# The second product of a streaming layer: x rounded ahead of the weights, block products in another order, the shared sum and the layer norm sums spread over more steps

## The chip, the cores and the metric

One core of one Trainium2 chip runs the kernel in one launch. The metric is the device time of that launch in microseconds, the median over runs of the same program.

## What is computed

One encoder layer over 1056 rows (1024 of a prompt, 32 of a running stream). The change concerns its last part, the second product of the MLP and the layer norm behind it. The reference, cut to that:

```python
x = _layernorm(ALPHA * x + mix, ln1_g, ln1_b)
hid = jax.nn.relu(x @ w_ff1)                    # (1056, 1024) @ (1024, 4096)
ff = (hid * hid) @ w_ff2                        # (1056, 4096) @ (4096, 1024)
x = _layernorm(ALPHA * x + ff, ln2_g, ln2_b)
```

Everything is float32. A float32 operand goes through TensorE as a rounded part and a remainder, and a product of two operands as three matmuls (`three`): rounded by rounded, rounded by remainder, remainder by rounded.

## The kernel before

**Block products.** The 4096 hidden features are 32 tiles of 128. Tiles 14, 15, 30 and 31 (`CLASSIC`) go through plain products. The other 28 make 14 pairs, and each pair's product with the weights is done as seven block products in place of eight (Winograd's form of Strassen's scheme). The weights of a pair are four blocks of 128 x 512, `A["11"]`, `A["12"]`, `A["21"]`, `A["22"]`; the columns are two halves of 528 (`H`), each two quarters of 264 (`Q`). The sums of hidden blocks that the seven products need were written to DRAM (`hd`) by the first product.

**Groups and steps.** `ff2_chunk` makes the steps of one group of pairs (groups of 5, 5 and 4). A product is one step for each pair: 4 tiles of outputs (d) by 2 quarters by 3 matmuls, 24 matmuls. The products stand in the order P1, P2, P6, P7, P4, P5, P3. P1 and P2 add into the same four accumulators (`acc`, two PSUM banks each; four of them are all that there are), P7 and P4 into the same four, P5 and P3 into the same four; P6 has four alone. P6 takes weights n2 = A21 + A22 - A11 (two additions, L1033 and L1034, which leave n1 and n2 behind), P7 takes A11 - A21, P3 takes A12 - n2 (one addition each, `add_w`, L853); P1, P2, P4 and P5 take blocks that are there.

**What a step has.** `load` (DMAs, all issued on SP's queue), `prep`, `mm` and `post`. `prep` of a product forms the weights on DVE, rounds them on ACT (L108) and takes the remainder on POOL (L111), then rounds the hidden block x on ACT and takes its remainder on DVE (L111). `post` of a product's last step takes the four accumulators out: `keep` adds them to the shared sum u (on DVE L1002; in the first group, for P1, a copy on ACT, L1000), `add_z` adds them to the output tiles `zz` (L1009, L1011). P1 and P6 go to u.

**The order of the work.** `run` writes the program out: at step i the loads of step i + 6, the preps up to step i + 3, then the matmuls and the post of step i. Each engine and SP's queue work through their own rows in exactly that order (`manual_schedule`). The rounded x lies in a ring of four slots, so the prep of step i + 3 waits for the matmuls of step i - 1; the rounded weights have six.

**The last group.** After P4 of the last group the program turns to quarters of columns: `qs[q]` are eight plain steps for quarter q (12 matmuls each), M5 is P5 in four steps (one for each d, 24 matmuls), M3 is P3 in two times four steps (12 matmuls each). They stand in the order qs[0], qs[1], M5, M3[0], qs[2], M3[1], qs[3]. `fold` adds u to three of the four quadrants of the output: quadrant (m, half) with m the half of the features. It stands in the posts of P7, one of the three additions on DVE and two on POOL. u's four parts lie in `w_b` and `w_c`; these tiles are used again afterwards for plain weights (`ew`) and for P3's.

**The second layer norm.** Quarters 0 to 2 use `ln2_parts`, whose pieces hang in the posts of later steps: `total` (three additions on POOL, L1225), `centre` (a small sum on TensorE, L1208, four subtractions on DVE, L1232, four squares on ACT and three additions on POOL, L1238), `root` (a small sum, L1208, then L1243 and L1244), and twice `scaled_out` (four of L1214 on DVE, four of L1215 on ACT, the output DMAs). Quarter 3 is `last_quarter`.

**Other lines that are spoken of:** `load_z` (L988) brings the tiles `zz` (1056 KB each) into buffers that `ff1_steps` used; L939 and L941 write the last sums of a pair of the first product to `hd`. L1126 and L1131 add the accumulators of M5 and M3, L1258 those of the plain steps.

Of the kernel before, what the change touches and what calls it, by code (L numbers as in the profile page):

```python
# [69 lines left out]
def hybrid_layer(ctx, tc, xT, win, wkw, wo, w1, w2, ckT, cv, ckiT, scT, cw, lnp, rb, cst, oh,  # L70
# [940 lines left out]
                    V.tensor_tensor(zs, accs[d], zs, op=OP.add)  # L1011
        return f

    def fold(d):

        def f():
            for i, (m, half) in enumerate(((1, 0), (1, 1), (0, 1))):
                zs = z_half(4 * m + d, half)
                (V if i == 0 else G).tensor_tensor(zs, zs, rings2["u"].parts[d], op=OP.add)
        return f  # L1020

    def ff2_chunk(ci, pairs):
# [14 lines left out]
        def product(loads, form, to, xn, post):  # L1037
            first = to.islower()
            to = to.lower()
            out = []  # L1040
            for i, p in enumerate(pairs):
                got = {}

                def load_x(p=p, got=got):
                    got["x"] = hidden_raw()
                    nc.sync.dma_start(got["x"], hd[p, FORM[xn]])

                def prep(p=p, got=got):
                    got["w"] = split_w(form(p))
                    hl = xhl.next().rearrange("p (a b) -> p a b", a=2)  # L1050
                    split(got["x"], hl[:, 0], hl[:, 1], lo_eng=V)
                    got["x"] = hl

                def mm(i=i, got=got):
                    if first and i == 0:
                        accs[to] = [new_acc() for _ in range(4)]
                    hl, x = got["w"], got["x"]
                    for d in range(4):
                        wh, wl = (hl[:, a, d * 128:d * 128 + 128] for a in range(2))
                        for c in range(2):  # L1060
                            cols = slice(c * Q, c * Q + Q)
                            three(accs[to][d][:, c], wh, wl, x[:, 0, cols], x[:, 1, cols],
                                  first and i == 0, i == len(pairs) - 1, not first)

                out.append(Step([load_a(n, p) for n in loads] + [load_x], [prep], [mm]))
            out[-1].post.append(lambda: post(accs[to]))
            return out

        def by_features(form, xn, place, post, groups):
# [9 lines left out]
            def prep(*ps):  # L1079
                def f():  # L1080
                    raw = [form(p) for p in ps]
                    for p, r in zip(ps, raw):
                        w, x = place(pairs.index(p))
                        split(r, *w)
                        split(got[p]["raw"], *x, lo_eng=V)
                        got[p]["w"], got[p]["x"] = w, x
                return f

# [39 lines left out]
        def post3(d, acc, cs):  # L1128
            for c in cs:
                zs = z_half(d, 1)[:, c * Q:c * Q + Q]  # L1130
                V.tensor_tensor(zs, acc[:, c], zs, op=OP.add)  # L1131

        P1 = product(["11"], lambda p: A["11", p], "a", "11", lambda a: keep(a, ci, True))
        P2 = product(["12"], lambda p: A["12", p], "A", "21", add_z(0, 0, ci == 0))
        P6 = product(["21", "22"], form_s2, "b", "t2", lambda a: keep(a, ci, False))
        P7 = product([], lambda p: add_w(A["11", p], A["21", p], OP.subtract), "c", "t3", add_z(1, 1, ci == 0))
        P4 = product([], lambda p: A["22", p], "C", "t4", add_z(1, 0, ci == 0))
        if ci == len(PAIRS) - 1:
            P5 = by_features(lambda p: n1[p], "t1", place5, post5, [(p,) for p in pairs])
            P3 = by_features(lambda p: add_w(A["12", p], n2[p], OP.subtract), "22", place3, post3, [pairs[:1], pairs[1:2], pairs[2:]])  # L1140
            return P1, P2, P6, P7, P4, P5, P3
# [76 lines left out]
    def ln2_parts(c0, n):  # L1218
        cols = slice(c0, c0 + n)
        got = {}  # L1220

        def total():
            got["s1"] = unit("s1")
            for i in range(1, 4):
                G.tensor_tensor(got["s1"], z[0][:, :, cols] if i == 1 else got["s1"], z[i][:, :, cols], op=OP.add)  # L1225

        def centre():
            mean = small_sum([(ones, got["s1"][:, a]) for a in range(2)])
# [11 lines left out]
        def root():  # L1240
# [2 lines left out]
            S.activation(got["rstd"], var, AF.Sqrt, bias=eps)  # L1243
            V.reciprocal(got["rstd"], got["rstd"])  # L1244

        return (total, centre, root, lambda: scaled_out(c0, n, got["rstd"], range(4)),
                lambda: scaled_out(c0, n, got["rstd"], range(4, 8)))

    def plain_step(q, d):
# [11 lines left out]
    def plain(q):  # L1261
        return [plain_step(q, d) for d in range(8)]
# [64 lines left out]
    n = len(steps)  # L1327
    for ci, pairs in enumerate(PAIRS):
        P1, P2, P6, P7, P4, P5, P3 = ff2_chunk(ci, pairs)
        steps += P1 + P2 + P6 + P7 + P4  # L1330
        if ci < len(PAIRS) - 1:
            steps += P5 + P3
    for i in range(4):
        steps[n + (2, 3, 8, 9)[i]].load.append(load_z(i))
    for j in range(8):
        load, prep = classic_x(j % 4, j // 4)
        steps[n + 36 + 4 * j].load.append(load)
        steps[n + 36 + 4 * j].prep.append(prep)
    for j in range(4):
        P7[j].post.insert(0, fold(j))  # L1340
    qs = [plain(0), plain(1), plain(2), last_quarter()]
    (load5, prep5, step5), (load3, prep3, step3) = P5, P3
    M5 = [step5(d, (0, 1)) for d in range(4)]
    M3 = [[step3(d, (c,)) for d in range(4)] for c in range(2)]
    steps += qs[0] + qs[1] + M5 + M3[0] + qs[2] + M3[1] + qs[3]
    for j in range(4):
# [4 lines left out]
        qs[0][5 + j // 2].load.append(load5[j])  # L1351
        qs[1][3 + j].prep.append(prep5[j])
        M5[1 + j // 2].load.append(load3[j])
    M5[3].prep += prep3
    for q, when in ((0, (qs[1][0], qs[1][3], qs[1][6], M5[0], M5[1])),
                  (1, (M5[0], M5[2], M3[0][1], qs[2][0], qs[2][2])),
                  (2, (M3[1][0], M3[1][3], qs[3][2], qs[3][4], qs[3][5]))):
        for f, st in zip(ln2_parts(q * Q, Q), when):
            st.post.append(f)
    with tc.manual_schedule(engines=ORDERED):  # L1360
# [84 lines left out]
```

## Time and profile before

| | |
|---|---|
| median of 3 runs | 1383.65 us (1382.64 to 1383.94) |
| the profiled execution: its own time, its span | 1387.17 us, 1385.4 us |
| PE busy | 1256.0 us, 91% of the span |
| DVE busy | 996.7 us, 72% |
| ACT busy | 691.6 us, 50% |
| POOL busy | 565.8 us, 41% |

The profile is of one execution. Times in it count from the start of its span, in microseconds. PE, DVE, ACT, POOL and SP are TensorE, VectorE, ScalarE, GpSimd and SyncE; L1002 is line 1002 of the kernel before. A wait is named by the instruction that waited and the one that released it. The granted clock of TensorE is given as a share of full speed (1.00 is 2.4 GHz, 0.50 is 1.2 GHz).

### The profile page before, as it was taken

The page shows a single profiled execution, that of the slowest core. Times are in us where ns is not written, and L with a number is a line of the kernel's source. Part 1 is how long each engine was busy: PE and PEld are TensorE (multiplying, and loading weights), DVE is VectorE, ACT ScalarE, POOL GpSimd, SP SyncE. Part 2 cuts the span into 40 slices and gives each one's busy share as a digit, 9 for nine tenths or more (in the row PEclk, how much of TensorE's full clock was granted, in tenths as well). Part 3 has the DMA queues.
Part 4 walks back from the last instruction along what each step waited for, and adds up shares of the span by engine and source line. Part 5 has one row for each costly group of instructions (what it writes and reads, how often), then busy time and mean ns, then how long its engine had stood idle before and what let it go on. Part 6 is the DMA issues. An engine that isn't in the chain of part 4 may idle for free. (4 is left out here: it accounts for less than half of the span.)

```text
span 1385.4 us, 24095 instructions
## 1 busy us (share of the span) xinstructions
PE 1256.0 (91%) x8822; PEld 1213.8 (88%) x8822; DVE 996.7 (72%) x2039; ACT 691.6 (50%) x1378; POOL 565.8 (41%) x456
## 2 busy tenths in 40 slices
PE   7999999898899979777999999999889989988794
PEld 6999999897788969666999999999889979978784
DVE  5675899999588898789276667667565665675666
ACT  5676989544688788755222221223333434333224
POOL 2412344432511333455344454554343434438522
PEclk9999999999999999997999999999999989999997
DMA  6320111135521212242143443447734724622111
GB/s 199 97 68 30 46 47 40 49 113 173 148 55 24 69 39 47 80 137 96 60 163 122 151 155 137 143 156 249 272 82 123 239 79 117 210 75 81 36 60 63
DMA packets 97223, 149.99 MB, mean 108 GB/s; under 512 B 12456, under 2 KB 41808, under 8 KB 97104
## 3 DMA queue, kind: packets, MB, share of 16 engines
q1 hardware_dynamic: 81664, 139.55, 31.2%
q0 software_dynamic: 9504, 4.33, 1.8%
q10 hardware_dynamic: 5936, 4.58, 1.2%
q8 instruction: 69, 1.13, 0.4%
q14 instruction: 50, 0.41, 0.1%
HBM read 105.41 MB, written 43.00 MB: 107 GB/s over the span
## 5 line engine op out<-in xcount | busy, mean ns | idle before, releaser
L111 POOL TENSOR_TENSOR whl<-wraw,whl 128x512 fp32r<-128x512 f32 (+1 forms) x184 | 247.7, 1351 | 459.8 <-ACT whl L108 434.5
L858 PE MATMUL acc<-b,whl 128*128 128x264 f32 x1088 | 317.2, 292 | 30.9 <-DVE w_b L1002 11.9
L859 PE MATMUL acc<-b,whl 128*128 128x264 f32 x1088 | 315.8, 290 | 0.0
L860 PE MATMUL acc<-b,whl 128*128 128x264 f32 x1088 | 314.0, 289 | 0.0
L858 PEld LDWEIGHTS acc<-b,whl 128*128 128x128 f32 x1088 | 211.1, 194 | 33.3 <-issue 30.2
L108 ACT ACTIVATE whl<-wraw 128x512 fp32r<-128x512 f32 (+1 forms) x184 | 113.3, 624 | 230.8 <-DVE wraw L853 200.0
L860 PEld LDWEIGHTS acc<-b,whl 128*128 128x128 f32 x1088 | 211.4, 194 | 0.0
L859 PEld LDWEIGHTS acc<-b,whl 128*128 128x128 f32 x1088 | 210.7, 194 | 0.1
L131 PE MATMUL mm<-xh,whl 128*128 128x384 f32 (+4 forms) x520 | 172.5, 332 | 15.5 <-ACT whl L108 5.6
L132 PE MATMUL mm<-area,whl 128*128 128x384 f32 (+4 forms) x552 | 182.4, 331 | 0.4 <-DVE area L111 0.4
L111 DVE TENSOR_TENSOR b<-xraw,b 128x528 fp32r<-128x528 f32 x94 | 104.7, 1117 | 103.3 <-ACT b L108 99.8
L133 PE MATMUL mm<-xh,whl 128*128 128x384 f32 (+4 forms) x520 | 170.0, 332 | 0.0
L441 ACT ACTIVATE junka<-s,cand 128x1024 bf16<-128x1024 f32 (+1 forms) x93 | 96.5, 1037 | 41.8 <-DVE cand L454 34.0
L131 PEld LDWEIGHTS mm<-xh,whl 128*128 128x128 f32 (+1 forms) x520 | 98.2, 189 | 19.3 <-issue 8.1
L132 PEld LDWEIGHTS mm<-area,whl 128*128 128x128 f32 (+1 forms) x552 | 104.3, 189 | 3.0 <-DVE area L111 0.8
L111 POOL TENSOR_TENSOR whl<-at,whl 128x512 fp32r<-128x512 f32 x56 | 79.0, 1420 | 53.9 <-ACT whl L108 53.9
L133 PEld LDWEIGHTS mm<-xh,whl 128*128 128x128 f32 (+1 forms) x520 | 97.6, 188 | 3.2 <-POOL whl L111 1.2
L108 ACT ACTIVATE b<-xraw 128x528 fp32r<-128x528 f32 x94 | 59.9, 638 | 65.9 <-PE acc L860 47.6
L443 DVE TENSOR_SCALAR_CACHE_REDUCE junk<-s,cand 128x384 bf16<-128x384 f32 (+1 forms) x124 | 80.3, 648 | 1.3
L858 PE MATMUL acc<-area,whl 128*128 128x264 f32 x240 | 68.4, 285 | 0.0
L859 PE MATMUL acc<-area,whl 128*128 128x264 f32 x240 | 68.1, 284 | 0.0
L860 PE MATMUL acc<-area,whl 128*128 128x264 f32 x240 | 68.0, 283 | 0.0
(310 smaller groups left out, 3317.9 us busy)
## 6 DMA issues: line engine op xcount, KB each, us to landing
hd<-ring SPq DMA_DIRECT2D x98, 264.0 KB, 2.1
xraw<-hd SPq DMA_DIRECT2D x98, 264.0 KB, 2.7
at<-in_w_dram SPq DMA_DIRECT2D x58, 256.0 KB, 3.7
wraw<-in_win_dram SPq DMA_DIRECT2D x52, 256.0 KB, 2.6
wraw<-in_wo_dram SPq DMA_DIRECT2D x40, 256.0 KB, 2.7
w_a<-in_w_dram SPq DMA_DIRECT2D x23, 256.0 KB, 3.5
w_c<-in_w_dram SPq DMA_DIRECT2D x19, 256.0 KB, 4.6
zz<-zd SPq DMA_DIRECT2D x4, 1056.0 KB, 9.1
```

Source lines behind the costliest of these rows:

```text
L108: S.activation(hi, raw, AF.Copy)
L111: (lo_eng or G).tensor_tensor(lo, raw, f32(hi), op=OP.subtract)
L131: PE.matmul(ps, wh[k], a, start=(k == 0), stop=False)
L132: PE.matmul(ps, wh[k], b, start=False, stop=False)
L133: PE.matmul(ps, wl[k], a, start=False, stop=(k == K - 1))
L441: S.activation(junk(R, N), s, AF.Sign, bias=c, scale=-1.0, accum_out=cnt[:R, i:i + 1])
L443: V.tensor_scalar(junk(R, N), s, c, -float(k), op0=OP.is_ge, op1=OP.add, accum_out=cnt[:R, i:i + 1])
L858: PE.matmul(ps, wh, xhi, start=start, stop=False, skip_group_check=more)
L859: PE.matmul(ps, wh, xlo, start=False, stop=False, skip_group_check=more)
L860: PE.matmul(ps, wl, xhi, start=False, stop=stop, skip_group_check=more)
```

## The change

In the preps x is rounded ahead of the weights. In the first two groups P6 moves behind P7 and P4, and the loads of A21 and A22 move from P6 to P7 and P4; the last group keeps its order. The first two output tiles are loaded three steps earlier. The additions of u to the output move from the posts of P7 to those of P4, and eight of the twelve are on DVE now (before four). `total` is cut into three pieces that hang in the quarter's own steps, the other layer norm pieces move by some steps, and the preps of P3 in the last group hang in three steps in place of one.

```diff
--- before.py
+++ after.py
@@ -1011,12 +1011,11 @@
                     V.tensor_tensor(zs, accs[d], zs, op=OP.add)
         return f
 
-    def fold(d):
+    def fold(d, m, half, eng):
 
         def f():
-            for i, (m, half) in enumerate(((1, 0), (1, 1), (0, 1))):
-                zs = z_half(4 * m + d, half)
-                (V if i == 0 else G).tensor_tensor(zs, zs, rings2["u"].parts[d], op=OP.add)
+            zs = z_half(4 * m + d, half)
+            eng.tensor_tensor(zs, zs, rings2["u"].parts[d], op=OP.add)
         return f
 
     def ff2_chunk(ci, pairs):
@@ -1046,10 +1045,10 @@
                     nc.sync.dma_start(got["x"], hd[p, FORM[xn]])
 
                 def prep(p=p, got=got):
-                    got["w"] = split_w(form(p))
+                    raw = form(p)
                     hl = xhl.next().rearrange("p (a b) -> p a b", a=2)
                     split(got["x"], hl[:, 0], hl[:, 1], lo_eng=V)
-                    got["x"] = hl
+                    got["x"], got["w"] = hl, split_w(raw)
 
                 def mm(i=i, got=got):
                     if first and i == 0:
@@ -1081,8 +1080,8 @@
                     raw = [form(p) for p in ps]
                     for p, r in zip(ps, raw):
                         w, x = place(pairs.index(p))
+                        split(got[p]["raw"], *x, lo_eng=V)
                         split(r, *w)
-                        split(got[p]["raw"], *x, lo_eng=V)
                         got[p]["w"], got[p]["x"] = w, x
                 return f
 
@@ -1130,12 +1129,13 @@
                 zs = z_half(d, 1)[:, c * Q:c * Q + Q]
                 V.tensor_tensor(zs, acc[:, c], zs, op=OP.add)
 
+        ends = ci == len(PAIRS) - 1
         P1 = product(["11"], lambda p: A["11", p], "a", "11", lambda a: keep(a, ci, True))
         P2 = product(["12"], lambda p: A["12", p], "A", "21", add_z(0, 0, ci == 0))
-        P6 = product(["21", "22"], form_s2, "b", "t2", lambda a: keep(a, ci, False))
-        P7 = product([], lambda p: add_w(A["11", p], A["21", p], OP.subtract), "c", "t3", add_z(1, 1, ci == 0))
-        P4 = product([], lambda p: A["22", p], "C", "t4", add_z(1, 0, ci == 0))
-        if ci == len(PAIRS) - 1:
+        P6 = product(["21", "22"] if ends else [], form_s2, "b", "t2", lambda a: keep(a, ci, False))
+        P7 = product([] if ends else ["21"], lambda p: add_w(A["11", p], A["21", p], OP.subtract), "c", "t3", add_z(1, 1, ci == 0))
+        P4 = product([] if ends else ["22"], lambda p: A["22", p], "C", "t4", add_z(1, 0, ci == 0))
+        if ends:
             P5 = by_features(lambda p: n1[p], "t1", place5, post5, [(p,) for p in pairs])
             P3 = by_features(lambda p: add_w(A["12", p], n2[p], OP.subtract), "22", place3, post3, [pairs[:1], pairs[1:2], pairs[2:]])
             return P1, P2, P6, P7, P4, P5, P3
@@ -1219,10 +1219,11 @@
         cols = slice(c0, c0 + n)
         got = {}
 
-        def total():
-            got["s1"] = unit("s1")
-            for i in range(1, 4):
+        def total(i):
+            def f():
+                got["s1"] = unit("s1")
                 G.tensor_tensor(got["s1"], z[0][:, :, cols] if i == 1 else got["s1"], z[i][:, :, cols], op=OP.add)
+            return f
 
         def centre():
             mean = small_sum([(ones, got["s1"][:, a]) for a in range(2)])
@@ -1243,7 +1244,7 @@
             S.activation(got["rstd"], var, AF.Sqrt, bias=eps)
             V.reciprocal(got["rstd"], got["rstd"])
 
-        return (total, centre, root, lambda: scaled_out(c0, n, got["rstd"], range(4)),
+        return (total(1), total(2), total(3), centre, root, lambda: scaled_out(c0, n, got["rstd"], range(4)),
                 lambda: scaled_out(c0, n, got["rstd"], range(4, 8)))
 
     def plain_step(q, d):
@@ -1327,18 +1328,23 @@
     n = len(steps)
     for ci, pairs in enumerate(PAIRS):
         P1, P2, P6, P7, P4, P5, P3 = ff2_chunk(ci, pairs)
-        steps += P1 + P2 + P6 + P7 + P4
         if ci < len(PAIRS) - 1:
-            steps += P5 + P3
+            steps += P1 + P2 + P7 + P4 + P6 + P5 + P3
+        else:
+            steps += P1 + P2 + P6 + P7 + P4
     for i in range(4):
-        steps[n + (2, 3, 8, 9)[i]].load.append(load_z(i))
+        steps[n + (-1, 0, 8, 9)[i]].load.append(load_z(i))
     for j in range(8):
         load, prep = classic_x(j % 4, j // 4)
         steps[n + 36 + 4 * j].load.append(load)
         steps[n + 36 + 4 * j].prep.append(prep)
     for j in range(4):
-        P7[j].post.insert(0, fold(j))
+        d = (j + 3) % 4
+        P4[j].post[:0] = [fold(d, 1, 0, V), fold(d, 1, 1, G)]
     qs = [plain(0), plain(1), plain(2), last_quarter()]
+    P4[0].post.append(fold(3, 0, 1, V))
+    for d in range(3):
+        P4[1 + d].post.insert(0, fold(d, 0, 1, V))
     (load5, prep5, step5), (load3, prep3, step3) = P5, P3
     M5 = [step5(d, (0, 1)) for d in range(4)]
     M3 = [[step3(d, (c,)) for d in range(4)] for c in range(2)]
@@ -1351,10 +1357,12 @@
         qs[0][5 + j // 2].load.append(load5[j])
         qs[1][3 + j].prep.append(prep5[j])
         M5[1 + j // 2].load.append(load3[j])
-    M5[3].prep += prep3
-    for q, when in ((0, (qs[1][0], qs[1][3], qs[1][6], M5[0], M5[1])),
-                  (1, (M5[0], M5[2], M3[0][1], qs[2][0], qs[2][2])),
-                  (2, (M3[1][0], M3[1][3], qs[3][2], qs[3][4], qs[3][5]))):
+    for f, st in zip(prep3, (M5[3], M3[0][0], M3[0][1])):
+        st.prep.append(f)
+    for q, when in ((0, (qs[1][2], qs[1][7], M5[0], M5[1])),
+                    (1, (M5[1], M3[0][3], qs[2][2], qs[2][5])),
+                    (2, (M3[1][1], qs[3][1], qs[3][2], qs[3][3]))):
+        when = (qs[q][3], qs[q][5], qs[q][7]) + when
         for f, st in zip(ln2_parts(q * Q, Q), when):
             st.post.append(f)
     with tc.manual_schedule(engines=ORDERED):
```

The ACT row, at the fourth and fifth step of the first group's P2 (b_6874 is the ring of rounded x, whl_6870 that of rounded weights, xraw_6872 the loaded x, w_b the loaded A12). Before:

```order
L108 ACTIVATE whl_6870<-w_b 128x512
L108 ACTIVATE b_6874<-xraw_6872 128x528
L1000 ACTIVATE w_b<-acc 128x528 x3
L1000 ACTIVATE w_c<-acc 128x528
L108 ACTIVATE whl_6870<-w_b 128x512
L108 ACTIVATE b_6874<-xraw_6872 128x528
```

Now:

```order
L108 ACTIVATE b_6874<-xraw_6872 128x528
L108 ACTIVATE whl_6870<-w_b 128x512
L1000 ACTIVATE w_b<-acc 128x528 x3
L1000 ACTIVATE w_c<-acc 128x528
L108 ACTIVATE b_6874<-xraw_6872 128x528
L108 ACTIVATE whl_6870<-w_b 128x512
```

In each prep the rounding of x has moved ahead of the rounding of the weights.

DVE's row in the last group, from P7's last steps to P4's (zz are output tiles, two features tiles each; L1019 and L1018 are the additions of u, L1011 the adding of accumulators, L111 the remainder of x). Before:

```order
L1019 TENSOR_TENSOR zz_10814<-zz_10814,w_b 128x528
L111 TENSOR_TENSOR b_6874<-xraw_6872,b_6874 128x528
L1019 TENSOR_TENSOR zz_10814<-zz_10814,w_b 128x528
L111 TENSOR_TENSOR b_6874<-xraw_6872,b_6874 128x528
L1019 TENSOR_TENSOR zz_10846<-zz_10846,w_b 128x528
L111 TENSOR_TENSOR b_6874<-xraw_6872,b_6874 128x528
L1019 TENSOR_TENSOR zz_10846<-zz_10846,w_c 128x528
L1011 TENSOR_TENSOR zz_10814<-acc,zz_10814 128x528 x2
L1011 TENSOR_TENSOR zz_10846<-acc,zz_10846 128x528 x2
L111 TENSOR_TENSOR b_6874<-xraw_6872,b_6874 128x528
```

Now:

```order
L111 TENSOR_TENSOR b_6874<-xraw_6872,b_6874 128x528
L1018 TENSOR_TENSOR zz_10846<-zz_10846,w_c 128x528
L1018 TENSOR_TENSOR zz_10547<-zz_10547,w_c 128x528
L1018 TENSOR_TENSOR zz_10514<-zz_10514,w_b 128x528
L1018 TENSOR_TENSOR zz_10814<-zz_10814,w_b 128x528
L1018 TENSOR_TENSOR zz_10514<-zz_10514,w_b 128x528
L1018 TENSOR_TENSOR zz_10814<-zz_10814,w_b 128x528
L1018 TENSOR_TENSOR zz_10547<-zz_10547,w_b 128x528
L1018 TENSOR_TENSOR zz_10846<-zz_10846,w_b 128x528
L1011 TENSOR_TENSOR zz_10814<-acc,zz_10814 128x528 x2
L1011 TENSOR_TENSOR zz_10846<-acc,zz_10846 128x528 x2
```

Four additions that stood between preps ahead of P7's post are eight now, in one piece, ahead of P4's post. POOL has four of the twelve now.

DVE's row at M5 (L1244 and L1245 are the reciprocals of a layer norm's root, at and w_b hold weights, area gets P3's rounded x). Before, from the reciprocal of quarter 0 on:

```order
L1244 RECIPROCAL at<-at 128x264
L1258 TENSOR_TENSOR zz_10846<-acc,zz_10846 128x264
L853 TENSOR_TENSOR wraw_6871<-w_b,at 128x512
L111 TENSOR_TENSOR area<-xraw_6872,area 128x528
L853 TENSOR_TENSOR wraw_6871<-w_b,at 128x512
L111 TENSOR_TENSOR area<-xraw_6872,area 128x528
L853 TENSOR_TENSOR wraw_6871<-w_b,at 128x512 x2
L111 TENSOR_TENSOR area<-xraw_6872,area 128x528 x2
L1126 TENSOR_TENSOR zz_10814<-acc,zz_10814 128x528
L1126 TENSOR_TENSOR zz_10608<-acc,zz_10608 128x528
L1214 SCALAR_TENSOR_TENSOR zz_10608<-zz_10608,lnw,at 128x264 x2
L1214 SCALAR_TENSOR_TENSOR zz_10640<-zz_10640,lnw,at 128x264 x2
```

Now, from the prep of P3's second pair on (L1125 is the line that was L1126, L1233 the one that was L1232):

```order
L853 TENSOR_TENSOR wraw_6871<-w_b,at 128x512
L111 TENSOR_TENSOR area<-xraw_6872,area 128x528
L1125 TENSOR_TENSOR zz_10814<-acc,zz_10814 128x528
L1125 TENSOR_TENSOR zz_10514<-acc,zz_10514 128x528
L1214 SCALAR_TENSOR_TENSOR zz_10814<-zz_10814,lnw,at 128x264 x2
L1214 SCALAR_TENSOR_TENSOR zz_10846<-zz_10846,lnw,at 128x264 x2
L1233 TENSOR_TENSOR zz_10514<-zz_10514,acc 128x2x264
L1233 TENSOR_TENSOR zz_10547<-zz_10547,acc 128x2x264
L1233 TENSOR_TENSOR zz_10814<-zz_10814,acc 128x2x264
L1233 TENSOR_TENSOR zz_10846<-zz_10846,acc 128x2x264
L853 TENSOR_TENSOR wraw_6871<-w_b,at 128x512 x2
L111 TENSOR_TENSOR area<-xraw_6872,area 128x528 x2
```

Before, all four preps of P3 (L853 and L111) stood ahead of M5's first post; now two pairs stand behind two posts, eight of L1214 and the centring of quarter 1.

## Rows read from the trace of the kernel before

**Rows 1.** Waits of PE, 990 to the end: total, times, longest, us

```profile
PE acc L858 <- DVE w_b L1002: 11.9, 3, 4.3
PE acc L858 <- DVE zz L1011: 11.2, 5, 4.4
PE acc L1208 <- POOL w_d L1225: 7.8, 1, 7.8
PE acc L1208 <- DVE w_d L1282: 6.4, 1, 6.4
PE acc L858 <- DVE zz L1009: 5.4, 1, 5.4
PE acc L1208 <- POOL w_d L1238: 5.2, 3, 2.2
```

**Rows 2.** Windows: length, busy PE, PEld, DVE, ACT, POOL, granted clock, DMA share, GB/s

```profile
1065.62:1109.76 44.14, 44.13 (x360) 43.93 (x360) 29.99 (x36) 18.08 (x32) 20.10 (x14) 1.00 0.70 222
...
1256.40:1262.25 5.85, 5.85 (x26) 5.85 (x27) 2.89 (x4) 0.00 (x0) 5.85 (x6) 0.50 0.00 0
sum 26.99, PE 26.98 PEld 26.99 DVE 19.03 ACT 5.08 POOL 9.12; mean PE 4.50 PEld 4.50 DVE 3.17 ACT 0.85 POOL 1.52
```

**Rows 3.** Timeline of the last group's P6 and P7 preps: start, duration, instruction

```profile
1214.33 0.69 DVE L1034 TENSOR_TENSOR at<-w_d,w_a 128x512 f32<-128x512 f32 x1
1216.32 1.37 DVE L111 TENSOR_TENSOR b<-xraw,b 128x528 fp32r<-128x528 f32 x1 [1.29 <-ACT b L108]
1218.32 0.69 DVE L1034 TENSOR_TENSOR at<-w_d,w_a 128x512 f32<-128x512 f32 x1
1231.28 0.68 DVE L853 TENSOR_TENSOR wraw<-w_a 128x512 f32<-128x512 f32 x1
1234.53 0.68 DVE L853 TENSOR_TENSOR wraw<-w_a 128x512 f32<-128x512 f32 x1
...
1215.12 0.63 ACT L108 ACTIVATE whl<-at 128x512 fp32r<-128x512 f32 x1 [2.82 <-DVE at L1034]
1215.66 0.63 ACT L108 ACTIVATE b<-xraw 128x528 fp32r<-128x528 f32 x1
```

**Rows 4.** Groups by line, 900 to the end: count, busy us, mean ns, idle before

```profile
L1034 DVE TENSOR_TENSOR at<-w_d,w_a 128x512 f32<-128x512 f32 x14 | 9.7, 692 | 0.5
L1011 DVE TENSOR_TENSOR zz<-acc,zz 128x528 f32<-128x528 f32 x36 | 23.3, 698 | 9.6 <-PE acc L860 7.7 <-POOL zz L1019 1.9
L1019 POOL TENSOR_TENSOR zz<-zz,w_c 128x528 f32<-128x528 f32 x2 | 2.6, 1308 | 0.0
L1244 DVE RECIPROCAL at<-at 128x264 f32<-128x264 f32 x3 | 5.4, 1803 | 10.3 <-ACT at L1243 10.3
L1214 DVE SCALAR_TENSOR_TENSOR zz<-zz,lnw,at 128x264 f32<-128x264 f32 x32 | 15.6, 552 | 0.0
```

**Rows 5.** Timeline of POOL and DVE at P7 of the last group

```profile
1242.88 3.55 POOL L1019 TENSOR_TENSOR zz<-zz,w_b 128x528 f32<-128x528 f32 x2
...
1243.42 1.83 DVE L1019 TENSOR_TENSOR zz<-zz,w_b 128x528 f32<-128x528 f32 x1
1245.17 1.82 DVE L111 TENSOR_TENSOR b<-xraw,b 128x528 fp32r<-128x528 f32 x1
```

**Rows 6.** Timeline of PE: the first matmul of the last group's P4

```profile
1256.40 0.56 PE L858 MATMUL acc<-b,whl 128*128 128x264 f32 x1 [4.43 <-DVE zz L1011]
```

**Rows 7.** Windows: the end of qs[1], and M5 to the first step of M3

```profile
1297.33:1299.79 2.46, 2.46 (x13) 2.46 (x12) 1.70 (x1) 0.48 (x1) 0.00 (x0) 0.50 0.00 0
1300.03:1323.97 23.94, 16.12 (x115) 15.49 (x114) 20.17 (x28) 10.12 (x19) 10.75 (x8) 0.86 0.13 46
```

**Rows 8.** Timeline of SP's queue: the last write of a pair, the first output tile

```profile
947.39 0.32 SPq L941 DMA_DIRECT2D hd<-ring  x1
953.33 0.43 SPq L988 DMA_DIRECT2D zz<-zd  x1
```

**Rows 9.** Chain of work that ended last: start, duration, link

```profile
972.91 9.07 DMA w_b<-in_w_dram
```

## Prediction

> **What bounds the kernel now.** I read the page's busy shares first, then the waits of TensorE, then the clock, then what the other engines do around each wait. TensorE's work is the same before and after, so only its waits and its clock can give time. In the stretch of the second product, from 990 on, it waits in two ways [rows 1]. Nine times the first matmul of a product waits for DVE to take an accumulator out (L1002, L1011, L1009): 11.9 + 11.2 + 5.4 = 28.5 us. Five times a small sum of the second layer norm waits (L1208): 7.8 + 6.4 + 5.2 = 19.4 us. The clock is the second thing to see: behind six of the nine waits TensorE works on at 1.2 GHz (granted clock 0.50) for 26.99 us in all [rows 2]. At 2.4 GHz 360 matmuls take 44.14 us, 0.1226 us each, so a step of 24 is 2.94 us; at half of that clock 27 us hold 13.5 us of such work, and 13.5 us are lost. With the waits that makes 42.0 us at product boundaries.
>
> Why is DVE late there? The preps of the next product stand ahead of the post in its row, and they are slower than the steps. From one L1034 to the next, in P6's preps, 3.99 us pass; from one L853 to the next, in P7's, 3.25 us [rows 3]; a step is 2.94. The rows between show the loop: DVE forms the weights, ACT rounds them (1215.12), then rounds x (1215.66, 0.63 us), and only then can DVE take x's remainder (1216.32, after 1.29 us of idling; 1.37 us long, as POOL has just begun on the weights). The next forming stands behind that.
>
> **x ahead of the weights.** DVE's operations stay; its idling on ACT goes, since x needs nothing of the forming. What is left of a prep on DVE is 0.69 + 0.70 = 1.39 us with one addition, 2.1 with two. Against POOL it may be more. L1019 and L111 on DVE take 1.83 and 1.82 us beside a busy POOL, with starts 1.75 us apart, and POOL's L1019 takes 3.55 us for two [rows 5]; alone such operations take about 0.69 on DVE and 1.31 on POOL [rows 4]. So the two take turns. With turns P6's prep needs 3 x 0.69 + 1.31 = 3.38 us, 0.44 more than a step, but only for the 5 (or 4) preps of P6, with three steps of lead; P7's needs 2.7 and keeps up. At a boundary the post then goes: step begins, x rounded 0.63, remainder 0.70, first accumulator 0.70, and 0.1 for each handing over (1214.33 + 0.69 to 1215.12): 2.3 us, within the step's 2.94, so the next product finds its accumulator. The lag of three P6 preps, 1.3 us, uses up the rest and some of the idle time before. I put the leftovers at 2.0 us in all: 0.2 at most boundaries, 0.6 and 0.8 at the two in the second group where a plain x is prepared in the same step (one more 0.70 on DVE). Bounds: nothing, and 2.5 us with its clock at four places (first rival).
>
> **The order of products and the loads.** The largest wait, 5.4 us, has DMAs behind it: a weight block of P2 took 9.07 us to land, beside the output tiles [rows 9]. P7 in P6's place needs five blocks fewer there, and two output tiles are moved away. They are moved past the loads of P1's first steps: SP's queue now issues the first right behind L941 at 947.39 (before at 953.33) [rows 8], ahead of P1's x and weights, and it waits there for the writes of that pair, as do all loads behind it. With three steps, 8.8 us, between load and prep I take 0.5 us; bounds 0 and 2.
>
> **The additions of u.** Eight in one piece on DVE. While P4 runs (4 x 2.94 = 11.8 us) POOL has the last weights of P4, four additions and four plain weights to do, nine operations, so DVE gets one turn in 1.75 us [rows 5]. DVE begins them 1.9 us into P4 (P7's post begins 1.6 us into its last step and takes 4 x 0.65, 23.3 / 36 in [rows 4], so it ends 1.2 over; then one remainder 0.70), ends 8 x 1.75 = 14.0 later, and gives the first accumulator 0.7 + 0.1 later: 16.7 us. qs[0] wants it at 11.8. So the 4.4 us wait at P4 [rows 6], counted above as gone, comes back as 4.9 us (16.7 - 11.8) at qs[0], and with it a half clock, taken as the mean of the six above, 13.5 / 6 = 2.2: together 7.1 us. Without turns the eight take 5.6 us and nothing waits: bounds 0 and 8.
>
> The Trainium skill, SBUF — State Buffer, section Who interferes with whom, says that a VectorE instruction with two inputs in SBUF and a GpSimd instruction that reads SBUF exclude each other for the whole instruction. It speaks against handing these additions to DVE, and the trace agrees (1.83 against 0.69); by the rule the wait at qs[0] is the 4.9, without it 0.
>
> **The layer norm pieces.** The three roots wait 5.2 us for POOL's squares [rows 1]. They stand one to two steps farther from their centrings now; I leave the last 0.5 and take 4.7, and 1.2 for the half clock behind the first (2.46 us [rows 7], half lost): 5.9. Quarter 1's total is on POOL ahead of P3's weights, so the 7.8 us wait goes from its place. But now the preps of P3's last two pairs stand behind more work on DVE: from M5's beginning 0.7 us for the root, the reciprocal 1.8, four formings and four remainders 5.5, four outputs of M5 2.8, eight of L1214 3.9 (15.6 / 32 each), four subtractions 2.8 [rows 4]: 17.5 us, and about five turns with POOL at 1.2: 23.5 us. M3's first step needs the last pair: it ends at 23.9 and then has about 1 us of half clock, where before 23.94 us passed [rows 7]. So this stretch loses 1.0; bounds -5 (no turns) and +4. Quarter 2's root comes a step (1.47 us) earlier, so that DVE's last queue, behind which the last sum waits 6.4 us, ends about 1.4 earlier. In all -5.9 + 1.0 - 1.4 = -6.3.
>
> **The sum.** -42.0 + 2.0 + 0.5 + 7.1 - 6.3 = -38.7 us. The profiled execution took 1387.17, so 1348.5 by its own time; it is 3.5 us above the median of the runs, 1383.65, and on that scale the forecast is 1345.0. A change of 0.2% (2.8 us) is about what a measurement of this kernel can tell from none.
>
> **The rivals.** (1) The turns with POOL keep the preps late: at the three boundaries before P6 and the last group's P7 a wait of 2.5 us and its 2.2 of clock stay, 18.8 us in place of some 1: 1363. For it: 3.38 us against 2.94. Against it: three steps of lead. (2) The turns cost little at the additions and at M5: 7.1 and 5 to 6 us less, 1332. For it: POOL waits for loads of plain weights at times. Against it: eight turns in a row, all of 1.75 us [rows 5]. (3) The change doesn't do what it says: what is late is loads and not ACT, and most waits move by a step; only a quarter of the 38.7 is gained: 1374. For it: the one 9.07 us load; against it: eight of the nine waits end on DVE's post behind idling on ACT. (4) It is slower: x waits for its slot, which the matmuls of three steps earlier free, and ACT in its fixed order can now round no weights before that. They are ready 0.63 + 0.63 + 1.31 = 2.6 us after the slot, with a forming behind a turn of POOL (1.83) 4.4; the lead is 8.8. Only if the chain passed 8.8 would each of the 82 product steps wait; from 0.47 us a step the 38.7 are gone, and at 0.7 it would take 1345 + 57 = 1402. Nothing in the rows comes near.
>
> **How the numbers follow.** Forecast 0.57 (1337 to 1353), (1) 0.17, (2) 0.14, (3) 0.07, (4) 0.05. The time is the first's, 1345. The range goes from (2) to (1) and leaves out (3), (4) and what lies beyond: 1332 to 1364. Faster is all but (4) and a part of (3) that gains next to nothing: 0.92; same 0.03; slower 0.05.
>
> **What would show it.** In the profile after, waits of TensorE for L1002, L1009 and L1011 should be gone but for fractions of a microsecond at P6 and P7, no half clock should stand between 990 and the last group's P4, and DVE's L111 should no longer idle 1.29 us on ACT. The first plain step should wait about 5 us for L1011, with L1018 at 1.8 us each; M3's first step should wait some 8 us for POOL or DVE, and no small sum but the last should wait over 1 us. I am wrong if P6's boundaries still wait 2 us or more, if L1018 takes 0.7, or if TensorE waits within products for rounded weights.

## The result, and the profile after

The changed kernel takes 1347.75 us (median of 4 runs, 1345.69 to 1348.35), the kernel before 1383.19 us in the same comparison (4 runs): a ratio of 0.9741, with an interval of 0.9724 to 0.9758. The forecast was 1345.0. The profiled execution took 1348.35 us, its span is 1346.6.

Some of the 38.8 us between the two spans isn't the change's. Everything ahead of the last stage of the first product is the same program, and it was 3.66 us shorter in this execution: the short wait of TensorE for L908, which stands in both kernels, ends at 942.38, before at 946.04. From there to the end the span of before has 439.4 us, that of after 404.2. The 35.1 us between these is what is explained here, and the medians differ by 35.4 (1383.19 - 1347.75). Line numbers of after are mostly one off those of before: L1018 is L1019 of before, L1033 is L1034, L1239 is L1238, L1283 is L1282.

The waits of TensorE after 930, all of them (engine, line, what it waited for: total, times, longest, us):

```profile
PE acc L1208 <- DVE w_d L1283: 6.1, 1, 6.1
PE acc L858 <- DVE zz L1011: 5.9, 3, 4.5
PE acc L858 <- ACT w L108: 5.1, 1, 5.1
PE acc L858 <- DVE ring L937: 3.0, 1, 3.0
PE acc L860 <- POOL w L111: 1.1, 2, 0.5
PE acc L858 <- ACT ring L908: 0.9, 1, 0.9
PE acc L1208 <- POOL w_d L1239: 0.5, 1, 0.5
PE acc L859 <- DVE area L111: 0.5, 1, 0.5
```

Against [rows 1] the two lines that stood for product boundaries in the groups are gone (L1002, L1009), and of L1011's three waits only 1.02 and 0.43 us belong to boundaries; the third, 4.48 us, is the first plain step. Together 23.1 us, before 49.6 with the two small ones ahead of 990. The clock, as windows around each half-clock stretch after 942 in which TensorE works (columns as in [rows 2]):

```profile
966.78:970.20 3.42, 3.42 (x18) 3.42 (x17) 1.21 (x2) 0.74 (x2) 1.52 (x1) 0.50 0.94 326
1233.02:1239.85 6.83, 5.12 (x23) 5.15 (x24) 3.84 (x6) 4.25 (x8) 6.83 (x6) 0.50 0.31 108
1280.81:1291.05 10.24, 8.21 (x31) 7.24 (x32) 6.40 (x8) 1.47 (x3) 4.31 (x3) 0.50 0.00 0
1328.60:1335.42 6.82, 3.23 (x7) 2.18 (x8) 4.15 (x12) 2.87 (x8) 0.06 (x1) 0.50 0.24 81
```

TensorE is busy at 1.2 GHz for 20.0 us in them, and half of that, 10.0 us, is lost; before, the same kind of windows hold 37.6 us of it, 18.8 lost. Waits 49.6 - 23.1 = 26.5 and clock 18.8 - 10.0 = 8.8 make 35.3 us: within 0.2 that is the whole difference. From 970.2 to 1233.0, from the first steps of P1 on through all three groups, the clock stays at 2.4 GHz.

DVE in the last group's P6, beside [rows 3] (timeline: start, duration, instruction):

```profile
1187.94 0.68 DVE L1032 TENSOR_TENSOR w_d<-w_a,w_c 128x512 f32<-128x512 f32 x1
...
1190.94 0.68 DVE L1032 TENSOR_TENSOR w_d<-w_a,w_c 128x512 f32<-128x512 f32 x1
1191.66 1.67 DVE L1033 TENSOR_TENSOR at<-w_d,w_a 128x512 f32<-128x512 f32 x1
1193.26 0.69 DVE L111 TENSOR_TENSOR b<-xraw,b 128x528 fp32r<-128x528 f32 x1
1193.88 2.54 DVE L1011 TENSOR_TENSOR zz<-acc,zz 128x528 f32<-128x528 f32 x4
```

A prep repeats every 3.0 us (1187.94 to 1190.94), before every 3.99, and DVE doesn't idle between its instructions. The remainder of x takes 0.70 us where it took 1.37. One addition of the prep takes its turn with POOL instead, at 1.67 where it took 0.69. So the turn has only moved, and what is gained is the idling of 1.29 us: -1.29 - 0.67 + 0.98 = -0.98, the whole of the 1.0 us. The remainders are shorter all over, 94 of them from 930 on (groups by line: count, busy us, mean ns, idle before; in the kernel before 104.7 us, 1117 ns each, with 103.3 us of idle time before them):

```profile
L111 DVE TENSOR_TENSOR b<-xraw,b 128x528 fp32r<-128x528 f32 x94 | 69.7, 742 | 87.1 <-ACT b L108 87.0
```

The first plain step, with the additions of u ahead of it (timelines of DVE, of POOL and of PE):

```profile
1220.07 3.56 DVE L1018 TENSOR_TENSOR zz<-zz,w_c 128x528 f32<-128x528 f32 x2
1223.55 10.41 DVE L1018 TENSOR_TENSOR zz<-zz,w_b 128x528 f32<-128x528 f32 x6
1233.89 2.54 DVE L1011 TENSOR_TENSOR zz<-acc,zz 128x528 f32<-128x528 f32 x4
...
1226.48 1.79 POOL L1018 TENSOR_TENSOR zz<-zz,w_b 128x528 f32<-128x528 f32 x1
1228.23 1.76 POOL L111 TENSOR_TENSOR ew<-w_d,ew 128x512 fp32r<-128x512 f32 x1
...
1234.73 0.56 PE L858 MATMUL acc<-area,ew 128*128 128x264 f32 x1 [4.48 <-DVE zz L1011]
```

Eight additions last 13.9 us, 1.73 us each from start to start (1220.07 to 1233.89), all in turn with POOL, whose two starts shown are 1.75 us apart. L1011 stands behind them, and TensorE's first plain matmul waits 4.48 us for its accumulator.

### The profile page after: what moved, and what is told of

It reads as the page before. It is cut to its first block, busy times and chain, and to the rows that moved or that the text cites. A ratio compares the mean times of both kernels' runs of the same rounds, so it can differ in the third digit from the quotient of the medians.

```text
span 1346.6 us, 24097 instructions
## 1 busy us (share of the span) xinstructions
PE 1245.1 (92%) x8822; PEld 1203.5 (89%) x8822; DVE 994.9 (74%) x2043; ACT 692.8 (51%) x1378; POOL 564.6 (42%) x452
## 5 line engine op out<-in xcount | busy, mean ns | idle before, releaser
L111 POOL TENSOR_TENSOR whl<-wraw,whl 128x512 fp32r<-128x512 f32 (+1 forms) x184 | 251.0, 1369 | 429.6 <-ACT whl L108 408.8
L858 PE MATMUL acc<-b,whl 128*128 128x264 f32 x1088 | 310.9, 286 | 6.1 <-DVE ring L937 3.0
L859 PE MATMUL acc<-b,whl 128*128 128x264 f32 x1088 | 310.7, 286 | 0.0
L860 PE MATMUL acc<-b,whl 128*128 128x264 f32 x1088 | 309.4, 284 | 0.0
L858 PEld LDWEIGHTS acc<-b,whl 128*128 128x128 f32 x1088 | 205.6, 189 | 7.1 <-DVE ring L937 3.2
L860 PEld LDWEIGHTS acc<-b,whl 128*128 128x128 f32 x1088 | 206.1, 189 | 0.0
L859 PEld LDWEIGHTS acc<-b,whl 128*128 128x128 f32 x1088 | 205.1, 189 | 0.1
L111 DVE TENSOR_TENSOR b<-xraw,b 128x528 fp32r<-128x528 f32 x94 | 69.7, 742 | 87.1 <-ACT b L108 87.0
L108 ACT ACTIVATE b<-xraw 128x528 fp32r<-128x528 f32 x94 | 60.5, 644 | 136.0 <-PE acc L860 82.1
L111 POOL TENSOR_TENSOR whl<-at,whl 128x512 fp32r<-128x512 f32 x56 | 81.5, 1465 | 30.8 <-ACT whl L108 30.8
L860 PE MATMUL acc<-area,whl 128*128 128x264 f32 x240 | 68.5, 286 | 0.0
```

The costliest lines, as they stand in the source:

```text
L108: S.activation(hi, raw, AF.Copy)
L111: (lo_eng or G).tensor_tensor(lo, raw, f32(hi), op=OP.subtract)
L858: PE.matmul(ps, wh, xhi, start=start, stop=False, skip_group_check=more)
L859: PE.matmul(ps, wh, xlo, start=False, stop=False, skip_group_check=more)
L860: PE.matmul(ps, wl, xhi, start=False, stop=stop, skip_group_check=more)
```

## The experiments

Each is compared with runs of the kernel before on the same chip: 1381.14 us (median of 8) for the first three, 1382.08 (9) for the last four. "From L908's wait" is again the span from the end of that wait, the part of the program in which they differ: 439.4 us before, 404.2 in the changed kernel.

**Where does the gain come from?** Three kernels take the change apart. The first is the changed kernel with the weights first again, in both preps:

```diff
-                    raw = form(p)
+                    got["w"] = split_w(form(p))
                     hl = xhl.next().rearrange("p (a b) -> p a b", a=2)
                     split(got["x"], hl[:, 0], hl[:, 1], lo_eng=V)
-                    got["x"], got["w"] = hl, split_w(raw)
+                    got["x"] = hl
```

> The changed kernel with the one edit of the preps undone: weights are rounded ahead of x again. Theory: the idling of DVE on ACT is what made the posts late, and the order of the products only moves the waits; so waits of 2.5 to 4.5 us with half clocks come back ahead of P6, P5 and, in the last group, P7 and P4, some 25 to 30 us in all: 1373 to 1378. Rival: the order of products and loads is what removed the waits; then it is at most 10 us slower, 1357 or less.

It took 1374.36 us (1372.91 to 1376.88), ratio 0.9951 [0.9935, 0.9967]; 430.6 us from L908's wait. Its waits from 985 to 1230:

```profile
PE acc L858 <- DVE zz L1011: 8.6, 6, 3.1
PE acc L858 <- DVE zz L1009: 3.1, 2, 2.4
PE acc L858 <- DVE w_b L1002: 3.0, 1, 3.0
```

Nine boundary waits stand in it, 14.7 us in all; the kernel before has 28.5 us, the changed kernel two waits of 1.45 together. The four of 2.4 us and more are ahead of P6 in each group and of P7 in the last; ahead of P5 and of the last P4, which the expectation also named, there is none. The idling that the prediction read in [rows 3] is back too; its timeline of DVE in the last group's P7:

```profile
1218.60 1.36 DVE L111 TENSOR_TENSOR b<-xraw,b 128x528 fp32r<-128x528 f32 x1 [1.30 <-ACT b L108]
...
1221.86 1.37 DVE L111 TENSOR_TENSOR b<-xraw,b 128x528 fp32r<-128x528 f32 x1 [1.29 <-ACT b L108]
```

The order inside a prep decides: 29.0 of the 35.4 us go with it (0.9951 - 0.9741 = 0.0210 of 1383 us, each ratio good to 0.0017). By the traces it is 26.4 us: about 20 at the product boundaries (13.2 of waits and 6.5 of clock), 3.7 at M5 and M3, whose prep has the same edit, and most of the rest behind L937.

The second is the kernel before with nothing but that order changed, in both preps; of the change's diff these pieces alone:

```diff
-                    got["w"] = split_w(form(p))
+                    raw = form(p)
...
-                    got["x"] = hl
+                    got["x"], got["w"] = hl, split_w(raw)
...
+                        split(got[p]["raw"], *x, lo_eng=V)
                         split(r, *w)
-                        split(got[p]["raw"], *x, lo_eng=V)
```

> The kernel before with that one edit alone: x rounded ahead of the weights, all else as before. Theory: seven or eight of the nine waits at product boundaries go with their half clocks (42 us less the one that has DMAs behind it, 5.4 + 1.7, and leftovers of 2, and the additions of u at P7 in place of P4, which keep some of their 4.4 + 2.9): 26 to 35 us less than before, 1348 to 1357. Rival: less than 15 us, since P6's two formings stand in the same places: above 1368.

It took 1348.74 us (1346.47 to 1350.07), ratio 0.9759 [0.9741, 0.9777]; 405.3 us from L908's wait. This reordering of a few lines gives nearly the whole change. Its waits at product boundaries, from 985 on:

```profile
PE acc L858 <- ACT ew L108: 2.3, 1, 2.3
PE acc L858 <- DVE zz L1011: 2.2, 1, 2.2
PE acc L858 <- DVE w_b L1002: 2.2, 1, 2.2
PE acc L858 <- DVE zz L1009: 1.0, 1, 1.0
```

The boundaries keep 7.7 us, and the layer norm most of its old waits (6.4 for L1282, 6.1 for L1225, 4.6 for L1238). Of the 7.7, 4.5 are at the last group's P4, behind the additions of u, which stand in P7's posts here as before: the 2.2 for L1011, and the 2.3 that the profile puts down to ACT's rounding of ew, while the first L1011 of that post begins at 1217.02 and the matmul at 1217.86. All the rest of the change alone is worth 0.49% (the first kernel), and on top of this one 0.0018 of ratio. Each ratio is good to 0.0017 or 0.0018, their difference to about 0.0025, so that isn't told from nothing. By the traces it is 1.1 us: the other parts gain 6.3 us of waits at the boundaries and 4.1 at the layer norm's roots, and lose 2.2 behind L937, 4.5 at the first plain step, 0.5 at M3 and 2.1 of clock, at the places that the last four kernels look at.

The third is the changed kernel with the products and the loads of A21 and A22 in their old order:

```diff
+        steps += P1 + P2 + P6 + P7 + P4
         if ci < len(PAIRS) - 1:
-            steps += P1 + P2 + P7 + P4 + P6 + P5 + P3
-        else:
-            steps += P1 + P2 + P6 + P7 + P4
+            steps += P5 + P3
```

> The changed kernel with P6 back behind P2 in the first two groups, with its double loads. Theory: the 9 us load of a weight block and the ten weight blocks of P6 make the wait behind the first P2, 5.4 us with 1.7 of half clock; it comes back in part or whole, and the second group loses at most 1 us: 4 to 8 us slower, 1351 to 1355. Rival: that wait, too, was DVE idling on ACT; then it is within 2 us of the changed kernel, 1346 to 1350.

It took 1347.58 us (1347.44 to 1347.89), ratio 0.9753 [0.9735, 0.977]; 405.3 us from L908's wait. My theory fell: the difference to the changed kernel's ratio, 0.0012, is within the intervals, and once x goes first the order of products is worth about 1 us in all (405.3 - 404.2). The timeline of DVE at the first P6 says why:

```profile
983.19 0.69 DVE L1032 TENSOR_TENSOR w_d<-w_a,w_c 128x512 f32<-128x512 f32 x1 [2.38 <-DMA w_c<-in_w_dram]
983.92 0.69 DVE L1033 TENSOR_TENSOR at<-w_d,w_a 128x512 f32<-128x512 f32 x1
...
985.23 0.69 DVE L1032 TENSOR_TENSOR w_d<-w_a,w_c 128x512 f32<-128x512 f32 x1
...
988.17 0.68 DVE L1032 TENSOR_TENSOR w_d<-w_a,w_c 128x512 f32<-128x512 f32 x1
...
991.10 2.53 DVE L1009 SCALAR_TENSOR_TENSOR zz<-zz,acc 128x528 f32<-128x528 f32 x4
```

The loads are as late as ever: DVE waits 2.38 us for a weight block, where it waited 2.08 in the kernel before. But from there three preps bring DVE to the post after 7.9 us (983.19 to 991.10), in the kernel before after 11.9 (986.72 to 998.66), and TensorE waits 0.84 us in place of 5.4. Late loads and slow preps make that wait together, and either remedy is enough: in the first kernel, with the weights first and the new order, the same boundary waits 0.72 us. So the two gains don't add.

The new order isn't without effect, though. In this kernel the boundaries cost 4.7 us, 0.84 here and 2.19 ahead of the second group's P7 with 3.41 us at half clock behind it; in the changed kernel they cost 1.45. That the whole differs by 1 us only is due to half clocks elsewhere, of which this execution lost 2.6 us less at places that the edit doesn't change: behind L937 it has none, though the wait there is 3.36 us. And the second group does lose more than the 1 us that I allowed it.

**What is left, and what does it cost?** Three kernels undo or move one thing each in the changed kernel. The first gives the first two output tiles their old places in SP's queue:

```diff
-        steps[n + (-1, 0, 8, 9)[i]].load.append(load_z(i))
+        steps[n + (2, 3, 8, 9)[i]].load.append(load_z(i))
```

> The changed kernel, with the loads of the first two output tiles back at the steps where they stood before. Theory: the early loads hold up P1's first loads, so P1's wait of 3.00 us for L937 falls to about 0.8 and the half clock of 3.41 us behind it (1.7 us lost) goes: 3.9 us less, 1343.8. Rival: the early loads are what lets P7's weights land in time; then the 5.4 us wait behind P2 is back with its half clock (1.7), and the time is about 1351.

It took 1344.37 us (1343.15 to 1346.4), ratio 0.9734 [0.9716, 0.9752]; 401.3 us from L908's wait, 2.9 fewer. By the times alone 0.0007 is nothing; the trace shows the mechanism. The wait behind P2 that the rival named didn't come back. Timelines of SP's queue, ACT, DVE, POOL and PE in the changed kernel, where the first tile is issued at 944.40, ahead of the loads of P1's first step, and the second at 946.32, ahead of those of its second step:

```profile
944.40 0.70 SPq L988 DMA_DIRECT2D zz<-zd  x1
...
956.88 0.65 ACT L108 ACTIVATE b<-xraw 128x528 fp32r<-128x528 f32 x1 [4.03 <-DMA xraw<-hd]
...
957.55 0.71 DVE L111 TENSOR_TENSOR b<-xraw,b 128x528 fp32r<-128x528 f32 x1 [1.75 <-ACT b L108]
958.91 1.07 DVE L928 SCALAR_TENSOR_TENSOR ring<-ring 128x528 f32<-128x528 f32 x1
960.02 1.69 DVE L929 TENSOR_TENSOR ring<-ring 128x528 f32<-128x528 f32 x1
961.75 1.67 DVE L931 TENSOR_TENSOR ring<-ring 128x528 f32<-128x528 f32 x1
...
958.12 4.72 POOL L111 TENSOR_TENSOR whl<-w_a,whl 128x512 fp32r<-128x512 f32 x3 [3.91 <-ACT whl L108]
...
965.32 0.39 PE L858 MATMUL acc<-b,whl 128*128 128x264 f32 x1 [3.00 <-DVE ring L937]
```

With the tiles at their old places the same rounding and the same matmul are:

```profile
949.07 0.65 ACT L108 ACTIVATE b<-xraw 128x528 fp32r<-128x528 f32 x1 [1.16 <-DMA xraw<-hd]
...
960.98 0.39 PE L858 MATMUL acc<-b,whl 128*128 128x264 f32 x1 [0.97 <-DVE ring L937]
```

With the tiles of 1056 KB ahead, x of the second step lands later: its load is issued at 948.25 and ACT can round it 8.6 us later, with the tiles at their old places 3.2 us (945.87 to 949.07), and there DVE takes its remainders without idling. Here DVE waits 1.75 us for it to be rounded, and then three of POOL's remainders come in a row: L928, L929 and L931 take 1.07, 1.69 and 1.67 us against 0.71, 0.71 and 1.72 without. The wait falls from 3.00 to 0.97 without the early tiles, and the half clock behind it is gone. Of these 2.0 us, 0.7 are there when DVE begins L927 (15.8 us after L908's wait in place of 15.1), and 1.3 come from there to L937 (6.4 us in place of 5.1).

The second moves six additions of u out of the way: three of POOL's to DVE, behind the posts of the plain steps, and three of DVE's there too.

```diff
-        P4[j].post[:0] = [fold(d, 1, 0, V), fold(d, 1, 1, G)]
+        P4[j].post[:0] = [fold(d, 1, 0, V)] + [fold(3, 1, 1, G)] * (j == 0)
...
-        P4[1 + d].post.insert(0, fold(d, 0, 1, V))
+        qs[0][1 + d].post.append(fold(d, 0, 1, V))
+        qs[0][4 + d].post.append(fold(d, 1, 1, V))
```

> The changed kernel, with six of the twelve additions of u (both right quadrants, features tiles 0 to 2 of each) moved from P4's posts to qs[0]'s, all six on DVE; P4 keeps five on DVE and one on POOL. Theory: the wait of 4.48 us at qs[0] comes from eight turns of DVE with POOL at 1.75 us; five turns end before P4 does (1.9 + 8.75 + 0.8 = 11.5 against 11.8), so the wait and its half clock (2.6 us lost) go: 7 us less, 1340.7. Rival: qs[0] waits for the plain weights' remainders on POOL and not for the additions; then at least 3 us of wait stay, now with POOL as the one who is waited for, and the time is above 1344. Six turns in qs[0] take DVE past its steps of 1.47 us for a while; if that is too much, a new wait of 2 to 3 us stands in qs[0].

It took 1340.63 us (1337.08 to 1345.9), ratio 0.9707 [0.9681, 0.9733]; 397.1 us from L908's wait, 7.1 fewer. Of L1011's waits only the two at boundaries are left, and no window has a half clock from 969.4 to 1273.1:

```profile
PE acc L858 <- DVE zz L1011: 1.5, 2, 1.0
```

The third moves half of quarter 0's scaled output and quarter 1's centring behind the preps of P3's last pairs:

```diff
-    for q, when in ((0, (qs[1][2], qs[1][7], M5[0], M5[1])),
-                    (1, (M5[1], M3[0][3], qs[2][2], qs[2][5])),
+    for q, when in ((0, (qs[1][2], qs[1][7], M5[0], M5[3])),
+                    (1, (M5[2], M3[0][3], qs[2][2], qs[2][5])),
```

> The changed kernel, with the centring of quarter 1 moved from M5's second step to its third, and the second half of quarter 0's output from the second step to the fourth, so that all preps of P3 stand ahead of both. Theory: M3's first step waits 6.7 us in all because P3's last two pairs are prepared behind these eight operations of DVE and three turns with POOL (1.65 + 2.5 + 3.6 = 7.7 us); now the wait is 1 us or less, and the half clock behind it (about 4 us lost) goes: some 9 us less, 1338. Rival: POOL's exclusion and the preps themselves are what is slow; then 4 us or more of the wait stay and the time is above 1344.

It took 1342.71 us (1339.56 to 1343.68), ratio 0.9716 [0.9697, 0.9736]; 397.7 us from L908's wait, 6.5 fewer. M3's first step no longer waits 5.10 us; what comes in its place is in these waits:

```profile
PE acc L1208 <- DVE zz L1130: 2.0, 1, 2.0
PE acc L860 <- POOL w L111: 1.0, 2, 0.7
...
PE acc L858 <- DVE zz L1233: 0.7, 1, 0.7
```

The stretch waits 3.8 us in place of 6.7, and TensorE is busy at half clock for 3.4 us in place of 8.2. From the first plain step to quarter 2's root 5.3 us less pass, 0.9 of them for a shorter half clock behind the first plain step, so the edit gives some 4.5 us, where I had expected 9. Of the rest of the 6.5, 1.5 isn't the edit's: in this execution no half clock follows L937's wait (2.94 us).

All three together:

> The three edits together. If their waits are independent, the gains add: 3.9 + 7 + 9 = 20 us less than the changed kernel, 1328. If they share a cause (DVE and POOL taking turns all the way from P4 to M3), the sum falls short by 5 us or more: 1333 and above.

It took 1331.67 us (1330.62 to 1333.75), ratio 0.9642 [0.9624, 0.9661], the fastest of all; 387.2 us from L908's wait, 17.0 fewer, where the three alone make 2.9 + 7.1 + 6.5 = 16.5. The sum doesn't fall short, so no sign of a shared cause; the 1328 isn't reached, since the third edit gives less than 9. By the times the three alone differ from the changed kernel's ratio by 0.0007, 0.0034 and 0.0025, each difference good to 0.0025 to 0.0031, so they tell little of each; the 0.0099 of all three (13.7 us) is clear. The clock is at 2.4 GHz from 655.5 to 1310.9. The two largest waits left, both in the tail:

```profile
PE acc L1208 <- DVE w_d L1283: 6.1, 1, 6.1
PE acc L1208 <- DVE zz L1130: 2.0, 1, 2.0
```

## Why the prediction was right, and where its sizes were off

**The boundaries** (forecast -42.0 + 2.0). Right, in place and in size: the nine waits of 28.5 us are 1.45 now, the 13.5 us of clock are gone, so -40.5. The two that are left are in the second group, as forecast, ahead of P4 and P6, 1.02 and 0.43 us, together 1.45 for 1.4. At the first the plain x is prepared right ahead of the post, and DVE's remainder of it takes 1.37 us for the 0.70 that I had put; at the second it stands a step earlier. Rival (1) fell: a prep of P6 with its turn takes 3.0 us, not 3.38, as DVE's second addition takes 1.67 with its turn, where I had put 0.69 + 1.31. One sign was put badly: DVE's L111 does still idle on ACT, 87.0 us from 930 on, not much less than the 99.8 of before. But of ACT's own idling before these roundings, 136.0 us, 82.1 end now with TensorE's matmuls that free the slot (L860; before 47.6): there x can't be rounded earlier, and DVE is ahead of TensorE. The idling that cost was the one behind the weights. And one of the nine waits was not ACT's, though rival (3) counts eight so: ahead of the last P4, with 4.43 us, DVE's row was full of turns with POOL for the additions of u. With x first alone 4.5 us of it stay; in the changed kernel it is gone because the additions moved.

**The order of the products and the loads** (part of the 42.0). No error in the sum, but one in the reasons: I put the 5.4 us wait down to the 9.07 us load and gave its going to the new order. With x first it falls to 0.84 in the old order too. What the new order buys beyond that at the boundaries is 3.3 us, most of it in the second group, which I hadn't named; on the whole kernel it doesn't show beyond 1 us.

**The early output tiles** (forecast +0.5, bounds 0 and 2). Mis-sized, and the largest miss: the wait for L937 grew by 2.24 us (0.76 to 3.00) and 1.7 us of clock came behind it, 3.9 in all. I had seen that the loads behind would wait, but took three steps of lead, 8.8 us, for cover. That lead isn't there: with the tiles at their old places ACT stands idle for x of the second step from 947.91 on, 2.0 us after its load is issued. What came late was that x, and it bunched POOL's remainders against DVE's operations. With 3.9 in place of 0.5 the forecast's sum would have been -35.3, the measured one; that it is the same to the tenth is luck, since the other terms are off by -0.5, -0.1 and +0.6 and cancel.

**The additions of u** (forecast +7.1). Right: 4.48 us of wait and half of 5.12 us, 7.04; the kernel without six of the twelve there is 7.1 us shorter. So rival (2) fell at this place. That the sum fits so closely is in part luck: the wait is 0.4 us less than forecast and its clock 0.4 more. The Trainium skill, SBUF — State Buffer, section Who interferes with whom, also says that a VectorE instruction with at most one input in SBUF, outside the two-port modes, doesn't contend with GpSimd; the trace agrees: the four L1011 at 1233.89, each with one input in an accumulator, take 2.54 us while POOL works throughout, 0.64 each, no more than the mean in [rows 4].

**The layer norm pieces** (forecast -6.3). -5.7, and each part has its sign: the roots' waits fell by 4.7 (5.2 to 0.5) as forecast, with 1.7 of clock for 1.2; M5 and M3 took 6.7 us of waits and 4.1 of clock in place of 7.8 and 1.8, so +1.2 for +1.0, which fells the other half of rival (2). The wait was not the 8 us for POOL or DVE that I named: 5.10 for ACT's rounding and 1.6 behind it, and the clock lost behind it was 4.1, not 1. The last sum's wait was mis-sized: 6.1, not 5.0, so this part gave -0.5 for -1.4. Quarter 2's root did come earlier, but now four L1214 run beside POOL's four L1276 and take 3.20 us, before 1.70.

**The sum** is -40.5 + 3.9 + 7.0 - 5.7 = -35.3, forecast -38.7. Rivals (3) and (4) fell with the first kernel: the order inside the prep does carry the gain, and outside M3 no matmul of the changed kernel waits for rounded weights. In rival (4) a count was wrong: groups of 5, 5 and 4 pairs have 35 + 35 + 20 = 90 product steps, not 82, so 0.43 us a step would have undone the gain, and 0.7 would have made 1408.

## What to carry to other kernels

When an engine idles in a loop for another that does two jobs for it, ask which of the two it really needs first; here a swap inside two preps gave nearly all that the whole reordering did. A late load costs only what the work behind it can't make up, so look at how fast the waiting engine catches up before moving the load. When work is moved to a free engine, count its turns with the neighbour in the same stretch, and spread it over steps rather than piling it at a boundary.

## What the runs showed of the hardware

DVE and POOL, both with operations that take turns queued, get one each in 1.73 us (1.69 to 1.76 from start to start), less than the 0.69 + 1.31 = 2.00 us of the two alone [rows 4]. An exclusion for the whole of both instructions would give the 2.00. DVE's three-operand operation with two tensors in SBUF stretches as well (L928 0.71 to 1.07, L1214 0.43 to 0.80); the reciprocal at 1263.40, with one, takes 1.80 us beside POOL's L1225, as in [rows 4].

The same wait doesn't always cost the same clock: behind the first plain step's 4.5 us TensorE was busy at 1.2 GHz for 5.12 us in one kernel and 3.41 in the one with the centring moved, a wait of 2.0 us for L1130 was followed by 3.4 us of half clock in that kernel and by none in the last, and a wait of 3 us for L937 by 3.4 in the changed kernel and by none in two others. A forecast of clock from a mean, as here 2.2 us a wait, is good to a microsecond or two each, and two traces that differ by a few microseconds have to be compared place by place.
